# Output projection one token tile at a time in both column halves, all weight units resident, normalisation on VectorE, late modulation moved into the feed-forward

## The chip, the core and the metric

The kernel runs on one core of a Trainium2 chip. The metric is the device time of one execution in microseconds. The engines are named as the profile names them: PE (TensorE's matmuls) and PEld (its weight loads), DVE (VectorE), ACT (ScalarE), POOL (GpSimd) and SP (SyncE, whose queue issues nearly all of the kernel's DMAs).

## What is computed

Two post-norm layers of a trunk over 640 tokens: 512 latent tokens and 128 context tokens. `D_MODEL` is 1024 and the feed-forward width `D_FF` is 2816. Cut to what matters here:

```python
def trunk_layer(x, mod, w_in, w_out, ..., ln_g, ln_b, w_ffn_in, w_ffn_out, ctx):
    shift_m, scale_m, gate_m, shift_f, scale_f, gate_f = jnp.split(mod.astype(x.dtype), 6, axis=-1)
    z = (x * (1 + scale_m) + shift_m) @ w_in
    o, k_c, v_c, s_d, s_h = token_mixers(z, ...)
    x = layer_norm(ALPHA * x + gate_m * (o @ w_out), ln_g[0], ln_b[0])
    gt, up = jnp.split((x * (1 + scale_f) + shift_f) @ w_ffn_in, 2, axis=-1)
    x = layer_norm(ALPHA * x + gate_f * ((jax.nn.silu(gt) * up) @ w_ffn_out), ln_g[1], ln_b[1])
    return x, k_c, v_c, s_d, s_h
```

`mod` is SiLU(cond) times `w_mod[l]` plus a bias: six vectors of 1024 numbers for a layer, one set for the latent and one for the context tokens. The change touches the stretch from `o @ w_out` to the start of the feed-forward, once in each layer.

## The kernel before

The 640 tokens are five tiles of 128 (`tau` 0 to 4). Every product is float32-like: a weight unit is loaded as `raw` (512 KB, a ring of three buffers in the pool `praw`), ACT casts its high part into `hl`, DVE forms the low part (`hl<-raw,hl`), and PE makes three passes (high x high, high x low, low x high). The ring of `hl` units has four buffers. A matmul, a cast or a DMA is put on its engine's queue by a scheduler, which reorders the program as written; each engine then runs its queue strictly in order. Which order came out can be listed, and is shown below.

**Output projection** (`pop`). A result tile is 128 tokens by 512 columns, so there are two column halves (`nh` 0 and 1) of five tiles. A half needs four weight units `us0` or `us1` (each two of the eight 128-row slabs `k`), and a tile is 24 matmuls. Before, half 0 runs first for all five tiles, in two goes of two units each; then half 1 runs tile by tile, with one step of `mods_late` ahead of each product.

**Residual and normalisation.** After each half of a tile, `residual` runs on DVE: `rt` = psum x gate, `r` = ALPHA x + `rt`, and the statistics `st`. After half 1 `ln_next` makes the modulated normalised rows `xma`. For tiles 0 to 2 (`SHARED[0][CUR[0]]` is 3 in both layers) ACT applies the statistics, DVE multiplies by the row vector `sc` and POOL adds the row vector `sh` in two halves; for tiles 3 and 4 DVE does all of it in two passes (lines 542 and 543). `ffn_T` then transposes `xma` on PE (`pta`), ACT and DVE write its high and low part to `xT`.

**Sums for the feed-forward.** The input product of the feed-forward is done by seven block products instead of eight on halves of the tokens (`HT` = 320) and of `D_MODEL`. It needs three sums of `xT` blocks, which `ffn_sums` makes in `fA` and `fS` (ACT, DVE and POOL) and stores in `SX`.

**Feed-forward.** For each of the 22 blocks `f`, `pair_a(f)` makes the gate products `pfa` from one weight unit (`gate_unit`), and `pair_b(f)` the others (`pfc`, `pfb`, `pfd`) from two loads, `g_` and `u_`, out of which POOL and DVE make the differences `t`. `AHEAD` = 4 gate blocks go ahead. The blocks come in parts (0-4, 4-8, ...), and after each part its output product `pfo` is added to `r`.

**Late modulation** (`mods_late`, line 1395). Vector 5 (`gate_f`) of this layer and, in layer 0, vector 0 of the next one are worked out here: eight `raw` loads of `w_mod` for a vector, and eight matmuls (`psm`, as the profile counts them) for a load. A step takes two loads.

## Time and profile before

| what | value |
|---|---|
| time, median of 3 runs | 2103.04 us (2100.37 to 2107.04) |
| profiled execution: its own time | 2098.58 us |
| span of its core | 2096.8 us |
| PE busy | 1915.2 us, 91% |
| PEld busy | 1681.5 us, 80% |
| DVE busy | 1440.6 us, 69% |
| POOL busy | 891.6 us, 43% |
| ACT busy | 791.2 us, 38% |
| granted TensorE clock, mean | 0.956 |

The profile is of one execution, whose time is 1.8 us above its span. Times in rows count from the start of the span. Layer 0's output projection begins at 531 us and its feed-forward's first output product at 682 us; layer 1's projection begins at 1558 us.

### The profile page before, as it was taken

What the parts mean: (1) busy time and instruction counts of PE and PEld (TensorE: products, weight loads), DVE (VectorE), ACT (ScalarE), POOL (GpSimd) and SP (SyncE); (2) the same over time, 40 slices, a digit from 0 to 9 for tenths busy, and PEclk for the clock granted to TensorE, in tenths of its full rate; (3) what the DMA queues carried; (4) which work ended last, traced back from release to release, by engine and by line L of the source; (5) the groups of instructions that cost most, each with busy time, mean ns of one, the idle gap of its engine ahead of it and who ended that gap; (6) DMA issues with size and microseconds to landing.
All of it is one profiled execution on the core that took longest, in us unless ns stands there. A gap on an engine that the chain in (4) does not pass through costs nothing. (4 is left out here: it accounts for less than half of the span.)

```text
span 2096.8 us, 37785 instructions
## 1 busy us (share of the span) xinstructions
PE 1915.2 (91%) x14914; PEld 1681.5 (80%) x14914; DVE 1440.6 (69%) x2516; ACT 791.2 (38%) x1564; POOL 891.6 (43%) x988
## 2 busy tenths in 40 slices
PE   7999997778988999999989999977799799999996
PEld 5988986657768899989989979755687779989895
DVE  5458534778588866667666784368857897667676
ACT  3542322647143334333336323135742434334331
POOL 0375234766142132435156924357642411432445
PEclk7999998899999999999999999989889999999998
DMA  9423215872653322222434342377235232223221
GB/s 303 112 74 123 90 64 149 225 221 74 211 181 89 114 81 91 71 81 81 133 94 131 108 135 67 102 186 231 87 130 159 84 111 91 71 81 97 76 76 76
DMA packets 243399, 249.36 MB, mean 119 GB/s; under 512 B 19370, under 2 KB 190358, under 8 KB 243222
## 3 DMA queue, kind: packets, MB, share of 16 engines
q1 hardware_dynamic: 221046, 227.27, 35.0%
q10 hardware_dynamic: 22176, 19.67, 3.6%
q8 instruction: 118, 1.93, 0.4%
q14 instruction: 59, 0.48, 0.1%
HBM read 218.72 MB, written 28.18 MB: 118 GB/s over the span
## 5 line engine op out<-in xcount | busy, mean ns | idle before, releaser
L176 DVE TENSOR_TENSOR hl<-raw,hl 128x1024 fp32r<-128x1024 f32 (+1 forms) x210 | 280.1, 1337 | 88.7 <-ACT hl L273 70.9
L173 PE MATMUL pfo<-hl,ha 128*128 128x512 f32 x1320 | 312.9, 395 | 1.5 <-ACT hl L273 0.8
L173 PEld LDWEIGHTS pfo<-hl,ha 128*128 128x128 f32 x1320 | 246.1, 187 | 60.7 <-DVE ft L176 1.2
L176 POOL TENSOR_TENSOR r<-r,ft 128x512 f32<-128x512 f32 x96 | 143.0, 1510 | 248.4 <-DVE ft L176 247.7
L176 POOL TENSOR_TENSOR t<-raw 128x512 f32<-128x512 f32 x44 | 67.9, 1543 | 338.7 <-DMA raw<-in_w_ffn_in_dram 145.4
L173 PE MATMUL pfa<-xT,hl 128*128 128x320 f32 x1056 | 175.3, 316 | 8.7 <-DVE ms L176 3.5
L273 ACT CAST hl<-raw 128x1024 fp32r<-128x1024 f32 (+2 forms) x122 | 125.5, 1036 | 147.8 <-DMA raw<-in_w_ffn_out_dram 45.9
L173 PE MATMUL pfc<-sx,hl 128*128 128x320 f32 x1056 | 172.2, 311 | 9.4 <-ACT hl L1550 8.2
L173 PEld LDWEIGHTS pfa<-xT,hl 128*128 128x128 f32 x1056 | 162.7, 193 | 12.4 <-ACT sx L1513 3.9
L173 PEld LDWEIGHTS pfc<-sx,hl 128*128 128x128 f32 x1056 | 160.4, 189 | 13.0 <-ACT hl L1550 9.0
L1550 ACT CAST hl<-raw 128x1024 fp32r<-128x1024 f32 x88 | 92.1, 1051 | 207.7 <-PE pfo L173 104.4
L173 PE MATMUL paq<-xT,hl 128*128 128x320 f32 x768 | 123.1, 317 | 0.6 <-ACT az L1238 0.6
L173 PE MATMUL pop<-hl,xT 128*128 128x512 f32 x480 | 118.0, 402 | 0.7 <-ACT ae_p L1131 0.7
L173 PEld LDWEIGHTS paq<-xT,hl 128*128 128x128 f32 x768 | 115.7, 190 | 3.4 <-issue 1.2
L173 PEld LDWEIGHTS pop<-hl,xT 128*128 128x128 f32 x480 | 89.6, 191 | 24.9 <-issue 4.7
L176 POOL TENSOR_TENSOR hK<-hK,hT 64x256 f32<-64x256 f32 x120 | 90.6, 755 | 33.4 <-PE ph L173 27.7
L176 DVE TENSOR_TENSOR ft<-pfo,lg 128x512 f32<-128x512 f32 x96 | 63.8, 683 | 55.5 <-PE pfo L173 44.1
L173 PE MATMUL pfd<-xT,h 128*128 128x320 f32 x528 | 87.7, 316 | 9.9 <-DVE u L176 9.9
L176 DVE TENSOR_TENSOR t<-raw,t 128x512 f32<-128x512 f32 x88 | 73.9, 840 | 33.1 <-POOL t L176 33.0
L173 PE MATMUL pbq<-xT,hl 128*128 128x320 f32 x576 | 89.9, 313 | 1.0 <-DVE hl L176 0.4
L173 PEld LDWEIGHTS pfd<-xT,h 128*128 128x128 f32 x528 | 81.4, 193 | 11.4 <-issue 8.7
L173 PE MATMUL pfb<-sx,hl 128*128 128x320 f32 x528 | 88.6, 310 | 0.6 <-DVE hl L176 0.6
(409 smaller groups left out, 4213.0 us busy)
## 6 DMA issues: line engine op xcount, KB each, us to landing
raw<-in_w_ffn_in_dram SPq DMA_DIRECT2D x96, 512.0 KB
raw<-in_w_mod_dram SPq DMA_DIRECT2D x80, 512.0 KB
raw<-in_w_in_dram SPq DMA_DIRECT2D x56, 512.0 KB
raw<-in_w_ffn_out_dram SPq DMA_DIRECT2D x44, 512.0 KB
pc<-in_w_mod_dram SPq DMA_DIRECT2D x8, 1024.0 KB
raw<-in_w_out_dram SPq DMA_DIRECT2D x16, 512.0 KB
qksc<-az SPq DMA_DIRECT2D x16, 320.0 KB
qkhi<-azs SPq DMA_DIRECT2D x16, 256.0 KB
```

The costliest lines, as they stand in the source:

```text
L173: nc.tensor.matmul(out, lhsT, rhs, start=start, stop=stop, **kw)
L176: return eng.tensor_tensor(out, a, b, op)
L273: A.copy(hl[:, 0, :kt * n], raw[:, :kt * n])
L1550: A.copy(tile_[:, 0, :n], raw)
```

## The change

- Half 0 takes one unit (`u0[:1]`) for all five tiles first. Then the loop goes tile by tile: the other three units of half 0 for tile `i`, and half 1 for tile `i - 1`.
- The four units of half 1 no longer wait for the four of half 0 to leave the `hl` ring: three of them are put in buffers `w0` to `w2`, whose memory the three sums `SX` take over afterwards. `SX` becomes three tiles, and `ffn_sums` runs for both pieces behind the last tile.
- The half-1 products have one more psum bank (`n=QQ + RR + PP1`); `mods_late` no longer has one of its own there.
- `mods_late` moves into the feed-forward: one step after each `pair_a` of the first four, then one after each `pair_b` (layer 0 has eight steps, layer 1 four).
- Two gate units instead of one are loaded ahead, behind tile 4's half 0.
- `SHARED[0]` becomes (0, 0): DVE alone does the normalisation of all five tiles, in two passes each.
- The feed-forward's `s` and `g` buffers and `xtra` are allocated ahead of `ha`.

```diff
--- before.py
+++ after.py
@@ -245,7 +245,7 @@
     AFFINE = ((V, V), (G, G))
-    SHARED = [(3, 3), 3]
+    SHARED = [(0, 0), 3]
@@ -267,7 +267,8 @@
         raw, _ = raw_unit(src, kt, n)
         seq = [x_ for x_ in HL["seq"] for _ in range(x_[2])]
         hp_, tag, n_ = seq[HL["i"] % len(seq)]
-        hl = hp_.tile([P, 2, 1024], F32R, tag=tag, bufs=n_, name="hl")
+        w_ = 4 * HT if tag[0] == "w" else 1024
+        hl = hp_.tile([P, 2, w_], F32R, tag=tag, bufs=n_, name="hl")
         HL["i"] += 1
         with behind():
             A.copy(hl[:, 0, :kt * n], raw[:, :kt * n])
@@ -1455,7 +1456,7 @@
         psum_banks(True)
-        psum_phase(n=QQ + RR + PP1[:1], m=PP1[1:], t=PP2)
+        psum_phase(n=QQ + RR + PP1, t=PP2)
         rc, rp = pool(f"R{l}", "right")
         r = [rp.tile([P, D], F32, name=f"r{l}_{tau}") for tau in range(NT)]
         st = [rp.tile([P, 2, 6], F32, name=f"st{l}_{tau}") for tau in range(NT)]
@@ -1464,15 +1465,16 @@
         lg = rp.tile([P, D], F32, name=f"lg{l}")
         lb_ = rp.tile([P, D], F32, name=f"lb{l}")
         hx, hxp = pool(f"hx{l}", "left")
-        SX = hxp.tile([P, 3, 2, 4, HT], F32R, name=f"sx{l}")
         sc_, sp = pool(f"S{l}", "left")
         fA = sp.tile([P, 4, HT], F32, name=f"fa{l}")
         fS = sp.tile([P, 4, HT], F32, name=f"fs{l}")
         HL["seq"], HL["i"] = [(phl, "hl", 4)], 0
         lc, lp = pool(f"L{l}", "left")
         WB[0] = 3
-        pre = [lp.tile([P, D], F32, tag=t_, name=f"{t_}{l}") for t_ in ("sc0", "sh0", "sc1", "sh1")]
-        gm = [lp.tile([P, D], F32, name=f"gm{l}_{j}") for j in range(2)]
+        pre, gm = [], []
+        for j in range(2):
+            pre += [lp.tile([P, D], F32, tag=f"{t_}{j}", name=f"{t_}{j}{l}") for t_ in ("sc", "sh")]
+            gm.append(lp.tile([P, D], F32, name=f"gm{l}_{j}"))
         def residual(ps, gate, x, rt, nh, stt):
             cs = slice(nh * 512, (nh + 1) * 512)
...
@@ -1533,15 +1535,6 @@
         rowload(None, ln_b[l, 0], None, lb_)
         rows = affine_rows(lp, l, 4, 3, pre)
         Wi, Wo = w_ffn_in[l], w_ffn_out[l]
-        pss = [psS("n", f"pop{l}_0_{tau}") for tau in range(NT)]
-        us0 = [(rowunit(w_out[l], 2 * i, 2, 0, 512), [2 * i, 2 * i + 1]) for i in (2, 3, 0, 1)]
-        for tau in range(NT):
-            gemm_N(pss[tau], 512, xT, tau, us0[:2], last=False)
-        for tau in range(NT):
-            gemm_N(pss[tau], 512, xT, tau, us0[2:], first=False)
-            residual(pss[tau], gm[tau >= LT][:, :512], r[tau], r[tau], 0, st[tau])
-        us1 = [(rowunit(w_out[l], 2 * i, 2, 512, 512), [2 * i, 2 * i + 1]) for i in (2, 3, 0, 1)]
-
         def load_col(c0, f):
             return raw_unit(Wi[:, c0 + f * P:c0 + f * P + P].rearrange("(k p) n -> p k n", p=P), KT, P)[0]
@@ -1563,24 +1556,45 @@
                 raws[f] = (g_, load_col(DFF, f))
             gts[f] = in_two(g_, 1024, hl_tile())
-        gate_unit(0)
-        late_m = mods_late()
+
+
+        def out_unit(i, nh):
+            return rowunit(w_out[l], 2 * i, 2, nh * 512, 512), [2 * i, 2 * i + 1]
+
+        pss = [psS("n", f"pop{l}_0_{tau}") for tau in range(NT)]
+        u0 = [out_unit(i, 0) for i in (2, 3, 0, 1)]
         for tau in range(NT):
-            for _ in range(2):
-                next(late_m, 0)
-            ps = psS("n", f"pop{l}_1_{tau}")
-            gemm_N(ps, 512, xT, tau, us1)
-            j = 0 if tau < LT else 1
-            residual(ps, gm[j][:, 512:], r[tau], r[tau], 1, st[tau])
-            AFTER[:] = ln_next(lp, r[tau], st[tau], mv, rs, rows[j], xT, tau, f"a{l}_{tau}", ffn_T)
-            if tau >= 3:
-                ffn_sums(*((0, 4 * P - HT) if tau == 3 else (4 * P - HT, HT)))
+            gemm_N(pss[tau], 512, xT, tau, u0[:1], last=False)
+        u1 = [out_unit(2, 1)]
+        HL["seq"], HL["i"] = [(hxp, f"w{x}", 1) for x in range(3)], 0
+        u1 += [out_unit(i, 1) for i in (3, 0, 1)]
+        HL["seq"], HL["i"] = [(phl, "hl", 4)], 0
+        for i in range(NT + 1):
+            if i < NT:
+                gemm_N(pss[i], 512, xT, i, u0[1:], first=False)
+                residual(pss[i], gm[i >= LT][:, :512], r[i], r[i], 0, st[i])
+            if i == NT - 1:
+                gate_unit(0)
+                gate_unit(1)
+            if i:
+                tau, j = i - 1, int(i > LT)
+                ps = psS("n", f"pop{l}_1_{tau}")
+                gemm_N(ps, 512, xT, tau, u1[1:] + u1[:1])
+                residual(ps, gm[j][:, 512:], r[tau], r[tau], 1, st[tau])
+                AFTER[:] = ln_next(lp, r[tau], st[tau], mv, rs, rows[j], xT, tau, f"a{l}_{tau}", ffn_T)
+        SX = [hxp.tile([P, 2, 4, HT], F32R, tag=f"w{x}", bufs=1, name=f"sx{l}_{x}") for x in range(3)]
+        ffn_sums(0, 4 * P - HT)
+        ffn_sums(4 * P - HT, HT)
         close(lc)
         close(sc_)
         psum_phase(g_n=PP1 + QQ + RR, t_m=PP2)
         fc, fp = pool(f"F{l}", "right")
+        ring = [[fp.tile([P, w_], F32, tag=f"{t_}{x}", bufs=1, name=f"{t_}{x}_{l}") for t_, w_ in (("s", HT), ("g", NTOK))]
+                for x in range(2)]
+        xtra = fp.tile([P, 2048], F32, tag="hb", bufs=1, name=f"xtra{l}")
+        ring += [[xtra[:, x * 960:x * 960 + HT], xtra[:, x * 960 + HT:x * 960 + 960]] for x in range(AHEAD - 2)]
         ha = fp.tile([P, 2, 4, NTOK], F32R, name=f"ha{l}")
         h_ = lambda xi, k: ha[:, xi, k]
         sc_, sp = pool(f"V{l}", "left")
...
@@ -1607,11 +1621,11 @@
             gt_ = gts.pop(f)
             a_ = psS("g", f"pfa{l}_{f}")
             prod(a_, gt_, 0, "11")
-            if 2 <= f < AHEAD:
-                s1, sg = xtra[:, (f - 2) * 960:(f - 2) * 960 + HT], xtra[:, (f - 2) * 960 + HT:(f - 1) * 960]
+            if f < AHEAD:
+                s1, sg = ring[f]
             else:
-                s1 = fp.tile([P, HT], F32, tag="s1", bufs=2, name=f"s1_{l}_{f}")
-                sg = fp.tile([P, NTOK], F32, tag="sg", bufs=2, name=f"sg{l}_{f}")
+                s1, sg = (fp.tile([P, w_], F32, tag=f"{t_}{f % 2}", bufs=1, name=f"{t_}{l}_{f}")
+                          for t_, w_ in (("s", HT), ("g", NTOK)))
             A.copy(s1, a_[:, :HT])
             prod(a_, gt_, 4, "12", start=False)
             A.activation(sg[:, :HT], a_[:, :HT], AF.Silu)
@@ -1659,14 +1673,16 @@
             A.activation(sg[:, HT:], u2, AF.Silu)
             return out(1, u4)
-        xtra = fp.tile([P, 2048], F32, tag="hb", bufs=1, name=f"xtra{l}")
+        late_m = mods_late()
         for f in range(AHEAD):
             pair_a(f)
+            next(late_m, 0)
         for part, (f0, f1) in enumerate(FF_PARTS):
             nk = f1 - f0
             last = part == len(FF_PARTS) - 1
             for f in range(f0, f1):
                 end = pair_b(f, f - f0)
+                next(late_m, 0)
                 if AHEAD - 1 <= f < NFF - 1:
                     pair_a(f + 1)
                 if part == 0:
```

Where instructions now stand is seen on three queues. On DVE in layer 0, these are the rows around the first use of a half-1 product (`rt<-pop_1_0`); the first number after `pop` is the half, the second the tile. Before:

```order
L176 TENSOR_TENSOR rt<-pop_0_3_6113,gm_0_6095 128x512
L1481 SCALAR_TENSOR_TENSOR r_3_6068<-r_3_6068,rt 128x512
L1482 BN_STATS st_3_6073<-r_3_6068 128x6
L176 TENSOR_TENSOR hl<-raw,hl 128x1024
L176 TENSOR_TENSOR rt<-pop_0_4_6114,gm_1_6096 128x512
L1481 SCALAR_TENSOR_TENSOR r_4_6069<-r_4_6069,rt 128x512
L1482 BN_STATS st_4_6074<-r_4_6069 128x6
L176 TENSOR_TENSOR hl<-raw,hl 128x1024
L176 TENSOR_TENSOR rt<-pop_1_0_6327,gm_0_6095 128x512
L1481 SCALAR_TENSOR_TENSOR r_0_6065<-r_0_6065,rt 128x512
L176 TENSOR_TENSOR rt<-pop_1_1_6407,gm_0_6095 128x512
L1482 BN_STATS st_0_6070<-r_0_6065 128x6
```

and now:

```order
L176 TENSOR_TENSOR rt<-pop_1_0_6228,gm_0_6092 128x512
L176 TENSOR_TENSOR rt<-pop_0_2_6111,gm_0_6092 128x512
L1483 SCALAR_TENSOR_TENSOR r_0_6065<-r_0_6065,rt 128x512
L1483 SCALAR_TENSOR_TENSOR r_2_6067<-r_2_6067,rt 128x512
L1484 BN_STATS st_0_6070<-r_0_6065 128x6
L176 TENSOR_TENSOR rt<-pop_1_1_6299,gm_0_6092 128x512
L1484 BN_STATS st_2_6072<-r_2_6067 128x6
L176 TENSOR_TENSOR rt<-pop_0_3_6112,gm_0_6092 128x512
L531 BN_AGGR mv_6075<-st_0_6070 128x2
L1483 SCALAR_TENSOR_TENSOR r_1_6066<-r_1_6066,rt 128x512
L1483 SCALAR_TENSOR_TENSOR r_3_6068<-r_3_6068,rt 128x512
L532 TENSOR_SCALAR rs_6076<-mv_6075 128x1
```

The residuals of half 0 for tiles 2, 3 and 4 stood ahead of the first half-1 residual; now they stand behind it, between the residuals of half 1 (tile 4's follows behind these rows), and `xma` is written by lines 543 and 544, which are lines 542 and 543 of before.

On PE in layer 1, these are the rows from the last of half 0's first tiles to the end of `pop_1_0`. Before:

```order
L173 MATMUL pop_0_3_16347<-hl,xT_14419 128x512 x12
L173 MATMUL pop_1_0_16561<-hl,xT_14419 128x512 x12
L173 MATMUL pop_1_1_16641<-hl,xT_14419 128x512 x6
L173 MATMUL pop_1_0_16561<-hl,xT_14419 128x512 x2
L173 MATMUL pop_1_1_16641<-hl,xT_14419 128x512 x4
L173 MATMUL pop_1_0_16561<-hl,xT_14419 128x512 x6
L173 MATMUL pop_1_1_16641<-hl,xT_14419 128x512 x5
L173 MATMUL pop_1_0_16561<-hl,xT_14419 128x512
L173 MATMUL psm_5_16536<-raw,cm 32x256 x4
L173 MATMUL pop_1_0_16561<-hl,xT_14419 128x512 x3
```

and now:

```order
L173 MATMUL pop_0_1_16337<-hl,xT_14412 128x512 x18
L173 MATMUL pop_1_0_16455<-hl,xT_14412 128x512 x12
L173 MATMUL pop_0_2_16338<-hl,xT_14412 128x512 x18
L173 MATMUL pop_1_1_16526<-hl,xT_14412 128x512 x12
L173 MATMUL pop_1_0_16455<-hl,xT_14412 128x512 x2
L173 MATMUL pop_1_1_16526<-hl,xT_14412 128x512 x2
L173 MATMUL pop_0_3_16339<-hl,xT_14412 128x512 x2
L173 MATMUL pop_1_0_16455<-hl,xT_14412 128x512 x10
L173 MATMUL pop_1_1_16526<-hl,xT_14412 128x512 x10
L173 MATMUL pop_0_3_16339<-hl,xT_14412 128x512 x16
L173 MATMUL pop_1_2_16597<-hl,xT_14412 128x512 x24
L173 MATMUL pop_0_4_16340<-hl,xT_14412 128x512 x4
```

All 120 matmuls of half 0 stood ahead of `pop_1_0`; now 16 of tile 3's and 4 of tile 4's stand behind it, and the modulation's `psm` is gone from there.

On SP in layer 0, these are the loads from the last unit of `w_out` to the first loads of `w_ffn_out`. Before:

```order
L254 DMA raw<-in_w_out_dram 128x2x512
L254 DMA raw<-in_w_ffn_in_dram 128x8x128
L254 DMA raw<-in_w_mod_dram 128x1024 x11
L482 DMA modrow_426<-ms_5_6403 4x256 x2
L470 DMA mbias<-in_b_mod_dram 4x256 x2
L254 DMA raw<-in_w_mod_dram 128x1024 x5
L254 DMA raw<-in_w_ffn_in_dram 128x8x128 x3
L482 DMA modrow_427<-ms_0_6564 4x256 x2
L470 DMA mbias<-in_b_mod_dram 4x256 x2
L254 DMA raw<-in_w_ffn_in_dram 128x8x128 x10
```

and now (10 of the rows that follow the same load):

```order
L254 DMA raw<-in_w_out_dram 128x2x512
L254 DMA raw<-in_w_ffn_in_dram 128x8x128 x2
L254 DMA raw<-in_w_mod_dram 128x1024 x4
L254 DMA raw<-in_w_ffn_in_dram 128x8x128
L254 DMA raw<-in_w_mod_dram 128x1024 x2
L254 DMA raw<-in_w_ffn_in_dram 128x8x128
L254 DMA raw<-in_w_mod_dram 128x1024 x2
L254 DMA raw<-in_w_ffn_in_dram 128x8x128 x2
L254 DMA raw<-in_w_mod_dram 128x1024
L483 DMA modrow_426<-ms_5_6765 4x256 x2
L471 DMA mbias<-in_b_mod_dram 4x256 x2
L254 DMA raw<-in_w_mod_dram 128x1024
```

The 16 loads of `w_mod` stood between the first gate unit's load and the other three; now they are spread between the gate units' loads and, after these rows, go on as two loads of `w_mod` to each two of `w_ffn_in`.

## Rows read from the trace of the kernel before

**Rows 1.** Busy time by stretch: us, PE, PEld, DVE, ACT, POOL, clock, DMA share, GB/s

```profile
531.00:571.20 40.20, 40.20 (x181) 31.86 (x182) 18.00 (x30) 6.34 (x14) 3.36 (x6) 1.00 0.65 223
571.20:629.20 58.00, 49.82 (x326) 36.02 (x326) 50.68 (x69) 22.92 (x34) 25.75 (x17) 0.94 0.58 182
594.30:629.20 34.90, 26.72 (x199) 20.11 (x199) 31.38 (x39) 16.70 (x27) 12.85 (x8) 0.90 0.69 212
1597.00:1654.70 57.70, 46.22 (x273) 35.75 (x271) 50.86 (x68) 22.91 (x35) 29.02 (x17) 0.96 0.37 110
1622.80:1654.70 31.90, 20.42 (x122) 18.15 (x120) 29.48 (x35) 15.99 (x27) 16.94 (x7) 0.93 0.27 76
```

**Rows 2.** PE's timeline: start, us, line, operation, result<-inputs, count, idle before it

```profile
548.23 21.94 PE L173 MATMUL pop<-hl,xT 128*128 128x512 f32 x93
570.10 0.64 PE L173 MATMUL psm<-raw,cm 128*32 128x256 f32 x8
...
631.82 0.56 PE L173 MATMUL pfc<-sx,hl 128*128 128x320 f32 x2 [1.46 <-ACT hl L1550]
...
681.99 22.67 PE L173 MATMUL pfo<-hl,ha 128*128 128x512 f32 x96 [0.79 <-ACT hl L273]
...
1656.48 0.90 PE L173 MATMUL pfc<-sx,hl 128*128 128x320 f32 x2 [6.76 <-ACT hl L1550]
```

**Rows 3.** DVE's timeline, in the same columns

```profile
550.46 0.69 DVE L1482 BATCH_NORM_STATS2 st<-r 128x6 f32<-128x512 f32 x1
...
571.21 0.69 DVE L176 TENSOR_TENSOR rt<-pop,gm 128x512 f32<-128x512 f32 x1 [6.95 <-PE pop L173]
571.94 0.69 DVE L1481 SCALAR_TENSOR_TENSOR r<-r,rt 128x512 f32<-128x512 f32 x1
...
588.17 1.21 DVE L176 TENSOR_TENSOR xma<-xma,sc 128x1024 f32<-128x1024 f32 x1
...
629.19 1.40 DVE L176 TENSOR_TENSOR t<-raw,t 128x512 f32<-128x512 f32 x2
...
1597.00 0.69 DVE L176 TENSOR_TENSOR rt<-pop,gm 128x512 f32<-128x512 f32 x1 [3.93 <-PE pop L173]
...
1654.66 1.41 DVE L176 TENSOR_TENSOR t<-raw,t 128x512 f32<-128x512 f32 x2
```

**Rows 4.** DVE's groups, 571.2 to 629.2: shapes, count | busy, mean ns | idle before

```profile
L176 DVE TENSOR_TENSOR hl<-raw,hl 128x1024 fp32r<-128x1024 f32 x4 | 6.0, 1489 | 0.0
L1481 DVE SCALAR_TENSOR_TENSOR r<-r,rt 128x512 f32<-128x512 f32 x5 | 4.5, 903 | 0.0
L176 DVE TENSOR_TENSOR xma<-xma,sc 128x1024 f32<-128x1024 f32 x3 | 4.0, 1330 | 0.8 <-ACT xma L536 0.8
L543 DVE SCALAR_TENSOR_TENSOR xma<-xma,rs,sh 128x1024 f32<-128x1024 f32 x2 | 2.6, 1282 | 0.4 <-POOL rs L176 0.4
```

**Rows 5.** The same view of DVE, 1597 to 1654.7

```profile
L176 DVE TENSOR_TENSOR xma<-xma,sc 128x1024 f32<-128x1024 f32 x3 | 4.8, 1603 | 2.3 <-ACT xma L536 2.3
```

**Rows 6.** The matmuls `psm` alone, up to the end of the last `pop`

```profile
570.00:594.30 24.30, 4.24 (x48) 1.17 (x48) 0.00 (x0) 1.00 0.40 130
1590.00:1622.80 32.80, 5.52 (x64) 1.49 (x64) 0.42 (x1) 1.00 0.48 149
```

**Rows 7.** SP's timeline: load issues

```profile
608.06 0.38 SPq L254 DMA_DIRECT2D raw<-in_w_ffn_in_dram  x1
...
630.66 0.37 SPq L254 DMA_DIRECT2D raw<-in_w_ffn_in_dram  x1
...
676.76 0.39 SPq L254 DMA_DIRECT2D raw<-in_w_ffn_out_dram  x1
```

**Rows 8.** ACT's timeline: the cast behind the first of these loads

```profile
613.48 1.05 ACT L1550 CAST hl<-raw 128x1024 fp32r<-128x1024 f32 x1 [0.61 <-DMA raw<-in_w_ffn_in_dram]
```

**Rows 9.** POOL's timeline

```profile
579.06 6.48 POOL L176 TENSOR_TENSOR xma<-xma,sh 128x512 f32<-128x512 f32 x4 [2.35 <-PE psm L173]
...
634.50 1.43 POOL L176 TENSOR_TENSOR t<-raw 128x512 f32<-128x512 f32 x1 [5.78 <-DMA raw<-in_w_ffn_in_dram]
```

More of the change, by code (lines that the diff above doesn't have):

```diff
@@ L1514, in two @@
                 tt(V, lo, src, hi.bitcast(F32), ALU.subtract)
-            two(s_, SX[:, 0, 0, :, a:b], SX[:, 0, 1, :, a:b])
+            two(s_, SX[0][:, 0, :, a:b], SX[0][:, 1, :, a:b])
             tt(G, f_, x(0, 0), f_, ALU.subtract)
@@ L1520, in ffn_sums @@
                 tt(V, s_, s_, x(xi, 0), ALU.subtract)
-            two(s_, SX[:, 1, 0, :, a:b], SX[:, 1, 1, :, a:b])
+            two(s_, SX[1][:, 0, :, a:b], SX[1][:, 1, :, a:b])
             two(f_, xT[:, 0, 0:4, HT + a:HT + b], xT[:, 1, 0:4, HT + a:HT + b])
@@ L1524, in ffn_sums @@
             tt(V, s_, s_, x(1, 4), ALU.add)
-            two(s_, SX[:, 2, 0, :, a:b], SX[:, 2, 1, :, a:b])
+            two(s_, SX[2][:, 0, :, a:b], SX[2][:, 1, :, a:b])
         S.dma_start(r[0], xin(l, 0))
@@ L1591, in tile_trunk @@
               "22": lambda xi, k: xT[:, xi, 4 + k, HT:], "s3": lambda xi, k: xT[:, xi, k, HT:],
-              "s1": lambda xi, k: SX[:, 0, xi, k], "s2": lambda xi, k: SX[:, 1, xi, k],
-              "s4": lambda xi, k: SX[:, 2, xi, k]}
+              "s1": lambda xi, k: SX[0][:, xi, k], "s2": lambda xi, k: SX[1][:, xi, k],
+              "s4": lambda xi, k: SX[2][:, xi, k]}
         def prod(ps, w, k0, x, start=True):
```

## The prediction, as written before the changed kernel had run

> **What bounds the kernel now.** The page says PE: 91% busy. That is an average, so the first view I read is the busy time of each engine over the stretches that the change touches [rows 1]. In the first of them (531 to 571 us) PE is busy all 40.2 us and DVE only 18.0. From 571.2 to 629.2 it is the other way: DVE works 50.7 of 58.0 us, and after the last `pop` product (594.3) 31.4 of 34.9, while PE has 26.7 and a granted clock of 0.90. Layer 1 shows the same: DVE 50.9 of 57.7, and at the end 29.5 of 31.9 against PE's 20.4 at 0.93.
>
> The timelines say where DVE's run begins and ends. It begins when `pop_1_0` ends: `rt` starts at 571.21 after 6.95 us idle (1597.00 after 3.93 in layer 1), and it ends with `t` at 629.19 (1654.66) [rows 3]. PE's `pfc`, the first product that needs the sums and the second weight units, follows at 631.82 and 1656.48, 2.6 and 1.8 us behind the start of that `t` [rows 2]. From the output product at 682 on PE runs on without a gap (96 matmuls in 22.67), so what is won or lost up to there stays in the end time. The stretch to look at is therefore the one from `pop_1_0` to `pfc`, DVE ends it, and before it DVE has some 22 us to spare.
>
> The profiled execution's own time is 2098.58 us, 4.5 below the median of the runs, inside what they spread over. I make the sum against the profile and carry the difference over to the median.
>
> **Resident units.** PE has no gap in the stretch where half 1 had to wait for half 0's units (40.2 of 40.2) [rows 1]: 93 matmuls take 21.94 us, 0.236 each, back to back [rows 2]. So the third bank and the resident units bring PE nothing there. Their effect is the order of the products.
>
> **Start of DVE's run.** In layer 0 six more `pop` matmuls stand ahead of the end of `pop_1_0` (1.4 us) and one load's `psm` less (0.64 [rows 2]): 572.1 instead of 571.2, +0.9 with rounding. In layer 1, 20 matmuls of half 0 and one of another product now stand behind it (21 x 0.236 = 5.0) and one load's `psm` (0.6): 1591.4 instead of 1597.0, −5.6.
>
> **DVE's work in the run.** *Residuals.* Those of half 0 for tiles 2, 3 and 4 lay in DVE's idle time before 571. DVE takes its queue in order, and now they stand behind `rt<-pop_1_0`, so that cover is gone: three times `rt`, `r` and `st` at 0.69 each [rows 3], +6.2 per layer. What is late next is the normalised rows, hence the transposes and the sums. *Normalisation.* For three tiles two passes at 1.28 [rows 4] take the place of one at 1.21 when alone [rows 3]: 3 x (2.56 − 1.21) = +4.0. In return ACT's pass and POOL's six half adds (four took 6.48 [rows 9]) go, and with them what DVE pays for running beside POOL. In layer 0 the `xma` pass takes 1.33 instead of 1.21 (x3: 0.33), `r` 0.90 instead of 0.69 (x5: 1.07), and the low part `hl` 1.49 where it is about 1.22 alone (x4: 1.08, an estimate from the `xma` pass of the same size) [rows 3, 4]: −2.5. In layer 1 the `xma` pass alone gives 3 x (1.60 − 1.21) = 1.2 [rows 5], and with a share for `r` I take −1.8. Sum: +7.7 in layer 0, +8.4 in layer 1.
>
> The Trainium skill, page "SBUF — State Buffer", section "Who interferes with whom", says that DVE and GpSimd share one pair of SBUF ports under an exclusive lock. By that rule each of the six POOL adds could hold a two-input DVE instruction for its whole length, which is the last rival below; the lengthening in the rows is far smaller than the adds are long.
>
> Put together for layer 0: 572.1 + 50.7 + 7.7 = 630.5 if no wait is left, +2.6 gives `pfc` at 633.1. Of the 7.3 us that DVE now idles in the run, 0.8 is for ACT's `xma`, which goes [rows 4], and about 2 are waits for `pop`, which the moved residuals fill; with the other 4.5 it is 637.6. For layer 1: 1591.4 + 50.9 + 8.4 = 1650.7, +1.8 gives 1652.5; its idle 6.8 loses the 2.3 of `xma` [rows 5] and 0.7, and with the remaining 3.8 it is 1656.3. I choose near the lower ends, since other ready work now stands beside those waits: 634 (+2) and 1653.5 (−3).
>
> **The loads.** `raw` has three buffers. A load lands 3.8 us after its issue when little else runs (630.66 [rows 7] to POOL's start at 634.50 [rows 9]) and 5.4 when much does (608.06 to 613.48 [rows 7, 8]). Behind the last transposes nine loads now have to pass (five of `w_mod`, two gate units, `g_` and `u_`): three turns of the ring. With 1 us of queueing and the cast or `psm` a turn is 5.5 to 7, and the last adds POOL's `t` (1.43), DVE's (0.7) and ACT's cast (1.05): about 631 in layer 0 counted from 608, 634 to 636 with slow landings. So loads and DVE nearly tie there; layer 1 is alike, at 1651 to 1656.
>
> In layer 0 vector 0's eight loads then stand in the turns of `pair_b`, two to each `f`. A load of `w_ffn_in` holds its buffer for 3.84 and the chain POOL, DVE, ACT (1.43 + 1.40 + 1.05) and 1 of queueing, about 9; one of `w_mod` for 5.5. Four of them through three buffers are (18 + 11) / 3 = 9.7 us, 38.7 for four blocks. Now `pfc` to the first `w_ffn_out` load is 45 us (631.8 to 676.76) [rows 2, 7]. That load now stands behind vector 0's sum and stores, some 3 to 6 us more: 42 to 45, no loss. With landings of 5.4 a block is 11.8 and it comes to 50 to 53: +5 to +8, with the gate loads +9. I take +3, nearer to the unloaded row, since that one is from this very place. PE's own cost of these `psm` (8 x 0.64 = 5.1) goes beside those turns.
>
> **Clock.** The clock is 0.90 to 0.93 where PE waits between the products [rows 1]. Without `psm` to fill these waits PE is idle longer there and I price +0.5.
>
> **Nothing.** The second gate unit ahead, the banks and the order of the pools cost no instruction; the gate unit's cast goes beside the products of `pop`. The scheduler also shifts a few instructions of layer 1's mixers, at PE's pace in both; unknown, ±3 for the range.
>
> **Sum.** +2 − 3 + 3 + 0.5 = +2.5: 2101.1 for the profiled execution, 2105.5 at the median; I round to 2105. With both lower ends and no loss in the turns it is 2101, with both upper ends 2116.
>
> **The rivals.** *Faster: PE leads.* If the tail behind the last `pop` depends on that product and not on DVE's sum of work, `pfc` follows it. Up to that point six loads' `psm` leave PE in layer 0 (48 matmuls, 3.8 us) and eight in layer 1 (64, 5.1) [rows 2, 6], and the tail stays as long as now: −8.9, and if the ring of loads hides vector 0's turns, 2103 − 8.9 = 2094. For it: PE is busy without a gap up to `pop_1_0`, and the third bank and resident units take every wait from the products. Against it: DVE's 31.4 of 34.9 behind the last product. It decides if DVE finds the three residuals' 6.2 us in waits, which now total 7.3 and 6.8.
>
> *Slower: the loads pace.* If landings are 5.4 us in both chains, `pfc` comes at about 635 (+3) and in layer 1 no earlier than now (0 instead of −3), and the turns cost 9, with the clock: about +13, 2117. For it: vector 0's loads stood where the ring had time, now each `pair_b` needs twice the loads through the same three buffers. Against it: DMA share is 0.6 to 0.7 before `pfc` but loads after it landed in 3.84. It decides if a block's turn goes over 11.5 us.
>
> *It does not bring anything.* Layer 0's later start and layer 1's earlier one cancel; that is my forecast.
>
> *Faster: the shared port.* If POOL's adds held DVE for their whole length, six of 1.6 us would be 9.7 per layer, against 2.5 and 1.8 counted above: another −15, about 2090. Against it are the same rows: `xma` lengthened by 0.1 to 0.4 only. The rule on the lock is the page "SBUF — State Buffer" as above.
>
> **How the numbers follow.** A measurement can tell about 0.3% (6.3 us) from no change. Forecast 0.45, all within it; loads pace 0.28, slower; PE leads 0.20 and the port 0.07, faster. The range runs from 2092 (a little under PE leads) to 2117 (loads pace) and takes in the mixers' ±3; outside lie most of the port's case and the half of the loads' case that is dearer, together about 0.2. The forecast's own range is 2099 to 2110.
>
> **What the profile after would show.** Right: DVE idle until about 572 and 1591 before `rt<-pop_1_0`, then residuals of both halves mixed; `pfc` some 103 us after layer 0's `pop` begins at 531 (101 now) and 3 earlier than now in layer 1; blocks of `pair_b` in layer 0 at about 11 us each with PE waiting for loads, and the first `pfo` some 5 us later than now. Wrong: DVE with clear waits between the last `pop` and `pfc` would speak for PE or loads instead of its sum of work; `pfc` before 628 for PE leads; `raw` named as the releaser on ACT and POOL ahead of every `pfc` for the loads. What would upset it all is a wait that I put at nothing, most likely of `hl` units for their ring at the start of the projection.

## The result, and the profile after

The changed kernel is slower: 2122.59 us (median of 6 runs, 2119.78 to 2129.89) against 2107.37 for the kernel before (6 runs, 2100.37 to 2112.76) on the same chips. The ratio is 1.0086, 95% interval [1.0063, 1.011], so some 18 us (the two medians differ by 15.2). That is above the range of the prediction (2092 to 2117), and above its slower rival, the loads' pace, at 2117.

The profiled execution took 2123.51 us. These rows of its trace are the matmuls of three products in each layer (count, ns at least/median/most, first and last start); the window was cut at 1100 us, so the first, third and fifth are layer 0's.

```profile
L173 PE MATMUL pop<-hl,xT x240: 388/394/796, 536.9 to 595.5; 128*128 128x512 f32 x120
L173 PE MATMUL pop<-hl,xT x240: 387/389/499, 1579.6 to 1636.0; 128*128 128x512 f32 x120
L173 PE MATMUL pfc<-sx,hl x528: 302/309/634, 643.8 to 1055.1; 128*128 128x320 f32 x176
L173 PE MATMUL pfc<-sx,hl x528: 302/309/637, 1679.9 to 2077.8; 128*128 128x320 f32 x176
L173 PE MATMUL pfo<-hl,ha x660: 387/394/793, 702.2 to 1078.2; 128*128 128x512 f32 x165
L173 PE MATMUL pfo<-hl,ha x660: 388/394/506, 1721.5 to 2102.3; 128*128 128x512 f32 x165
```

From them I take two lengths for each layer, which all experiments below are read by: from the first `pop` to the first `pfc` (layer 0: 643.8 − 536.9 = 106.9; before 100.8), and from there to the last `pfo` (layer 0: 434.4; before 424.5). Layer 1 went from 98.9 to 100.3 and from 420.9 to 422.4. Together these are +18.9 us, about the 18 of the ratio. Ahead of layer 0's first `pop` both kernels run the same instructions in the same order, and the 5.9 us between 531.0 and 536.9 are of these two executions (last section). Between layer 0's last `pfo` and layer 1's first `pop` stand layer 1's token mixers, 501.3 us before and 501.4 now. Their instructions are the same, but the scheduler put about a quarter of DVE's 685 there at another place in the queue, and the 18 kernels of the table below have 14 different orders there. One sign of it: the five `hK` of one pass ran in one go on DVE before (first row) and now have another instruction among them (the next three):

```profile
1390.21 3.44 DVE L607 TENSOR_SCALAR hK<-hf 128x512 f32<-128x512 f32 x5 [0.78 <-DMA aks<-qksc]
```

```profile
1416.61 2.05 DVE L608 TENSOR_SCALAR hK<-hf 128x512 f32<-128x512 f32 x3
1418.59 0.14 DVE L1135 RECIPROCAL ari<-ar 128x1 f32<-128x1 f32 x1
1418.65 1.50 DVE L608 TENSOR_SCALAR hK<-hf 128x512 f32<-128x512 f32 x2
```

That stretch has a column of its own in the table below.

Where layer 0's 6 us ahead of `pfc` are is seen in DVE's timeline, around the start and the end of its run:

```profile
579.57 1.29 DVE L176 TENSOR_TENSOR rt<-pop,gm 128x512 f32<-128x512 f32 x2 [14.52 <-PE pop L173]
580.77 1.28 DVE L1483 SCALAR_TENSOR_TENSOR r<-r,rt 128x512 f32<-128x512 f32 x2
...
585.70 1.28 DVE L543 SCALAR_TENSOR_TENSOR xma<-r,mv,sc 128x1024 f32<-128x1024 f32 x1
...
636.60 0.69 DVE L176 TENSOR_TENSOR sx<-fs,sx 128x512 fp32r<-128x512 f32 x1 [2.12 <-ACT sx L1515]
638.45 0.42 DVE L176 TENSOR_TENSOR ms<-psm,mbias 128x256 f32<-128x256 f32 x1 [1.17 <-PE psm L173]
642.02 2.37 DVE L176 TENSOR_TENSOR t<-raw,t 128x512 f32<-128x512 f32 x2 [3.14 <-POOL t L176]
```

The run starts 42.7 us after the first `pop` (before 40.2) and has its last sum done at 637.3, 100.4 after it. Until there DVE waits 3.2 us in all. Then it waits 3.14 us for POOL, and POOL's own row says for what: a load.

```profile
640.73 1.26 POOL L176 TENSOR_TENSOR t<-raw 128x512 f32<-128x512 f32 x1 [15.42 <-DMA raw<-in_w_ffn_in_dram]
```

Layer 1 has the same wait, longer. DVE's last sum and its `t`:

```profile
1669.54 0.69 DVE L176 TENSOR_TENSOR sx<-fs,sx 128x512 fp32r<-128x512 f32 x1
...
1678.10 2.36 DVE L176 TENSOR_TENSOR t<-raw,t 128x512 f32<-128x512 f32 x2 [5.53 <-POOL t L176]
```

In the kernel before, `t` at 629.19 followed DVE's sums without a wait [rows 3]. Why the load comes late, SP's queue tells, its issues and then what it waited for from 560 to 643 us (total, times, longest):

```profile
559.87 4.44 SPq L254 DMA_DIRECT2D raw<-in_w_ffn_in_dram  x2
565.07 53.19 SPq L254 DMA_DIRECT2D raw<-in_w_mod_dram  x4
618.37 1.64 SPq L254 DMA_DIRECT2D raw<-in_w_ffn_in_dram  x1
...
633.90 2.69 SPq L254 DMA_DIRECT2D raw<-in_w_ffn_in_dram  x2
```

```profile
SPq L254 <- DVE hl L176: 51.9, 6, 44.9
SPq L254 <- PE psm L173: 16.0, 7, 6.0
```

Both gate units sit in `raw` and wait for their low parts on DVE. So SP stands still for 44.9 us behind the first load of `w_mod`, and the second and third go out 15 us after the last `pop`:

```profile
610.37 1.46 SPq L254 DMA_DIRECT2D raw<-in_w_mod_dram  x2
```

The windows show it as a DMA share of 0.00 (the columns are those of [rows 1]):

```profile
578.00:595.70 17.70, 17.70 (x77) 14.19 (x76) 16.13 (x27) 0.00 (x0) 3.04 (x2) 1.00 0.00 1
595.70:643.80 48.10, 33.00 (x209) 25.59 (x207) 40.55 (x52) 20.79 (x33) 15.52 (x9) 0.78 0.43 132
```

Behind `pfc` the blocks of layer 0 go to 702.18 instead of 681.99 [rows 2]. PE's last row there and SP's queue ahead of it:

```profile
702.18 1.22 PE L173 MATMUL pfo<-hl,ha 128*128 128x512 f32 x2 [5.14 <-ACT hl L274]
```

```profile
682.46 2.58 SPq L254 DMA_DIRECT2D raw<-in_w_ffn_in_dram  x2
689.48 0.34 SPq L515 DMA_DIRECT2D aff<-modrow  x1
...
694.59 1.07 SPq L483 DMA_DIRECT2D modrow<-ms  x2
695.70 0.53 SPq L471 DMA_DIRECT2D mbias<-in_b_mod_dram  x1
696.33 0.84 SPq L515 DMA_DIRECT2D aff<-modrow  x2
697.34 0.39 SPq L254 DMA_DIRECT2D raw<-in_w_ffn_out_dram  x1
```

The rows for layer 1 (`aff`, made in buffers of the same `raw` ring) need vector 0. Its store `modrow<-ms` is issued at 694.59, they wait for it, and the first load of `w_ffn_out` goes out behind them, 53.5 us after `pfc` (before 45 [rows 2, 7]). These small transfers, from the first `aff` at 689.48 to that load at 697.34, are called the chain below; they take SP 7.9 us. In the kernel before the chain stood there too, from 665.33 to 676.76, but vector 0 was long done.

### The profile page after: what moved, and what is told of

Same layout as the page of the kernel before. It is cut to its first block, busy times and chain, and to the rows that moved or that the text cites. A ratio compares the mean times of both kernels' runs of the same rounds, so it can differ in the third digit from the quotient of the medians.

```text
span 2121.7 us, 37750 instructions
## 1 busy us (share of the span) xinstructions
PE 1935.8 (91%) x14914; PEld 1698.8 (80%) x14914; DVE 1439.0 (68%) x2516; ACT 783.9 (37%) x1558; POOL 871.4 (41%) x976
## 5 line engine op out<-in xcount | busy, mean ns | idle before, releaser
L176 DVE TENSOR_TENSOR hl<-raw,hl 128x1024 fp32r<-128x1024 f32 (+1 forms) x210 | 274.2, 1311 | 92.1 <-ACT hl L274 71.2
L173 PEld LDWEIGHTS pfc<-sx,hl 128*128 128x128 f32 x1056 | 161.8, 191 | 15.2 <-ACT hl L1543 10.5
L1543 ACT CAST hl<-raw 128x1024 fp32r<-128x1024 f32 x88 | 92.2, 1051 | 209.2 <-PE pfo L173 102.2
L176 POOL TENSOR_TENSOR hK<-hK,hT 64x256 f32<-64x256 f32 x120 | 90.8, 757 | 40.1 <-PE ph L173 34.4
L173 PEld LDWEIGHTS pbq<-xT,hl 128*128 128x128 f32 x576 | 87.5, 194 | 2.6 <-issue 0.8
## 6 DMA issues: line engine op xcount, KB each, us to landing
raw<-in_w_ffn_in_dram SPq DMA_DIRECT2D x96, 512.0 KB
raw<-in_w_mod_dram SPq DMA_DIRECT2D x80, 512.0 KB
raw<-in_w_in_dram SPq DMA_DIRECT2D x56, 512.0 KB
raw<-in_w_ffn_out_dram SPq DMA_DIRECT2D x44, 512.0 KB
raw<-in_w_out_dram SPq DMA_DIRECT2D x16, 512.0 KB
```

Source lines behind the costliest of these rows:

```text
L173: nc.tensor.matmul(out, lhsT, rhs, start=start, stop=stop, **kw)
L176: return eng.tensor_tensor(out, a, b, op)
L1543: A.copy(tile_[:, 0, :n], raw)
```

## The experiments

Each kernel ran with the kernel before on the same chip, five rounds. The table stands first, since the texts point to it; times are us from the profiles as above, the ratio is to the kernel before with its 95% interval.

| kernel | L0 pop to pfc | L0 pfc to last pfo | L0 last pfo to L1 pop | L1 pop to pfc | L1 pfc to last pfo | ratio |
|---|---|---|---|---|---|---|
| before | 100.8 | 424.5 | 501.3 | 98.9 | 420.9 | 1 |
| changed | 106.9 | 434.4 | 501.4 | 100.3 | 422.4 | 1.0086 [1.0063, 1.011] |
| e1, modulation back | 106.3 | 423.2 | 497.5 | 102.2 | 421.8 | 0.9999 [0.9985, 1.0013] |
| e2, shared normalisation back | 107.0 | 433.6 | 498.8 | 104.0 | 423.4 | 1.0075 [1.0047, 1.0102] |
| e3, before + modulation moved | 99.0 | 433.8 | 510.3 | 101.9 | 422.6 | 1.0053 [1.0035, 1.007] |
| e4, before + DVE normalisation | 102.1 | 423.6 | 501.9 | 99.0 | 421.2 | 0.9992 [0.9976, 1.0008] |
| e6, no loads of w_mod | 103.7 | 422.5 | 504.4 | 95.7 | 421.6 | 0.9987 [0.9972, 1.0001] |
| e7, a quarter of psm | 104.6 | 429.8 | 491.9 | 100.2 | 423.7 | 1.0011 [0.9996, 1.0025] |
| e8, vector 0 in blocks 4 to 7 | 106.7 | 439.8 | 501.5 | 101.5 | 422.5 | 1.0113 [1.0099, 1.0127] |
| e10, and vector 5 back | 101.5 | 439.3 | 506.0 | 100.0 | 422.5 | 1.0109 [1.0094, 1.0123] |
| e11, rows a part later | 105.2 | 425.7 | 507.8 | 100.8 | 421.2 | 1.0043 [1.003, 1.0056] |
| f1, e3 + rows later | 100.8 | 426.2 | 497.0 | 100.0 | 421.9 | 1.0016 [1.0001, 1.003] |
| f2, before + rows later | 104.4 | 421.9 | 502.1 | 99.9 | 422.7 | 0.9986 [0.9975, 0.9997] |
| e12, modulation in the mixers | 97.5 | 423.9 | 505.0 | 96.3 | 421.2 | 0.9981 [0.9967, 0.9996] |
| e13, before + vector 0 in the mixers | 99.3 | 424.3 | 500.2 | 99.4 | 422.2 | 0.9981 [0.9968, 0.9995] |
| e14, before + modulation in the mixers | 98.5 | 422.9 | 512.0 | 96.7 | 422.6 | 1.004 [1.0026, 1.0054] |
| e15, vector 5 in pop, 0 in the mixers | 102.7 | 423.6 | 507.9 | 96.4 | 422.2 | 1.004 [1.0023, 1.0057] |
| f3, e12 + rows later | 97.7 | 422.9 | 499.0 | 92.8 | 420.9 | 0.997 [0.9954, 0.9987] |

How far to trust one profile: the kernel before and f2 run the same instructions in the same order up to the first `pfc` and show 100.8 and 104.4 in the first column. A difference under 4 us in the columns up to `pfc` says little. In the third column, layer 1's mixers, four pairs of kernels have the same order, but for two or three instructions at most: before and e4, e1 and e13, e2 and f1, e6 and e8. Within a pair the column differs by 0.6 to 2.9 us, over all kernels by 20 (491.9 to 512.0). Part of that is the execution, since layer 0's mixers differ by up to 10 us with one order (last section). So the order in layer 1's mixers may change the time by some us, which no run tests by itself, and a ratio can hold that without the change itself being its cause. The second column lies within 421.9 to 426.2 for every kernel but those that load vector 0 right ahead of the rows made of it, which are at 429.8 to 439.8.

**Which part of the change costs.** Theory L: the loads of the moved modulation. Theory D: the order of the residuals and the normalisation on DVE. Four kernels undo or do one part.

e1, the modulation put back:

```diff
-        psum_phase(n=QQ + RR + PP1, t=PP2)
+        psum_phase(n=QQ + RR + PP1[:1], m=PP1[1:], t=PP2)
...
             if i:
                 tau, j = i - 1, int(i > LT)
+                for _ in range(2):
+                    next(late_m, 0)
                 ps = psS("n", f"pop{l}_1_{tau}")
...
             pair_a(f)
-            next(late_m, 0)
```

> The changed kernel with the late modulation put back into the projection (two steps ahead of each half-1 product, its own psum bank). Theory L (the loads of w_mod now pass the ring of three behind the gate units and pace pfc and the first blocks): 2107 us, at the kernel before, and from the first pfc to the first pfo of layer 0 about 50 us again. Theory D (the order of residuals and the normalisation on DVE cost the time): stays above 2117.

e2, `SHARED = [(3, 3), 3]` in the changed kernel:

> The changed kernel with ACT, DVE and POOL sharing the normalisation of tiles 0 to 2 again. Theory L: no change against the changed kernel, 2120 to 2124. Theory D: 4 us back in each layer, 2114. If the shared port is what matters the time goes up by some 5 us, to 2127.

e3, the kernel before with the lines of `mods_late` as in the change and nothing else of it:

> The kernel before with the late modulation alone moved into the feed-forward (and its psum bank given to the half-1 products). Theory L: 2120, the whole loss, and layer 0's pfc to pfo about 58 us. Theory D: 2107, no loss.

e4, `SHARED = [(0, 0), 3]` in the kernel before:

> The kernel before with the normalisation by DVE alone. Theory L: 2107, no change. Theory D: 2113 to 2116, slower by half of the loss. Shared port: faster, 2098 to 2102.

e1 is back at the kernel before (0.9999), e2 stays with the changed one, e4 is no different from the kernel before. By the times theory D falls and theory L stands: the move of the modulation costs 11 us alone (e3) and 18 in the new order (changed against e1). The stretches say it less plainly. Between the profiles of the changed kernel and e1, 11.2 us come back behind `pfc` in layer 0 (434.4 to 423.2) and 3.9 in layer 1's mixers, but ahead of `pfc` in layer 0 nothing does (106.3). There DVE ends the stretch in e1: its `t` follows the last sum without a wait for a load.

```profile
637.28 1.41 DVE L176 TENSOR_TENSOR t<-raw,t 128x512 f32<-128x512 f32 x2
```

So the 6 us ahead of `pfc` are not the moved loads alone. With the old order the first column is 99.0 and 100.8 when the modulation is moved (e3, f1); with the new order it is 101.5 to 107.0 wherever loads of `w_mod` stand near it, 97.5 and 97.7 when all stand in the mixers (e12, f3), and 103.7 in e6 below, without the loads. Why the new order takes these loads worse is not shown. SP's long wait for the gate units is not the reason by itself: e12 has one of 41.8 us in its 97.5 (the view from 545 to 640 us).

```profile
SPq L254 <- DVE hl L176: 67.2, 7, 41.8
```

**Loads or PE's time.** e6 keeps the matmuls and drops the loads, e7 keeps the loads and drops most matmuls.

```diff
-                raw, _ = raw_unit(w_mod[l][k * P:(k + 1) * P, i * D:(i + 1) * D].unsqueeze(1), 1, D)
+                raw = late if late is not None else raw_unit(w_mod[l][k * P:(k + 1) * P, i * D:(i + 1) * D].unsqueeze(1), 1, D)[0]
...
-            yield from modulation(l, (5,))
+            yield from modulation(l, (5,), lb_)
```

> The changed kernel, whose late modulation makes all its matmuls but loads nothing: each reads the resident row of ln_b in place of a load of w_mod, so gate_f of each layer and the first shift of layer 1 are other numbers. If the loads in the ring of three are the cost: 2103 to 2107, layer 0's pfc to pfo at 50 us. If PE's time for these matmuls is the cost: 2118 to 2122. If the order of the residuals costs the 6 us ahead of pfc in layer 0, that part stays (107 us from the first pop to the first pfc) whatever the loads do.

```diff
-                for g in range(4):
+                for g in range(4 if late is None or k == 0 else 1):
```

> The changed kernel with all loads of w_mod, but seven of eight loads of a late vector feed one matmul of four, so three quarters of the late modulation's result hold one load's part of the sum only. If the loads are the cost: 2120 to 2123, no change. If PE's time is: 24 loads at 0.64 us, of which 21 keep a quarter, give 10 us back: 2112.

Without the loads the kernel is at 0.9987, all of the loss gone, and layer 1 is 3 us better than before ahead of `pfc`. So PE's 15 us of `psm` cost nothing by themselves (24 loads at 0.64). But e7 is at 1.0011, where theory L said no change, and that expectation failed. Its stretches give back some 7 us in layer 0 and nothing in layer 1. The rest of its 16 us shows where the edit does not reach: layer 1's mixers, in another order, took 491.9 where the changed kernel has 501.4. So 9.5 us of it may be that order and not the matmuls. That the matmuls matter while the loads are there fits SP's rows: a load's buffer comes free only when its `psm` has run, in PE's strict order. For the second load of a step in a block this was 655.97 (issue) to 663.95 (end of `psm`), 8 us, where I had put 5.5.

```profile
655.97 0.34 SPq L254 DMA_DIRECT2D raw<-in_w_mod_dram  x1
```

```profile
661.10 0.63 PE L173 MATMUL psm<-raw,cm 128*32 128x256 f32 x4
661.65 1.74 PE L173 MATMUL pfd<-xT,hl 128*128 128x320 f32 x10
663.32 0.63 PE L173 MATMUL psm<-raw,cm 128*32 128x256 f32 x4
```

**Where vector 0 stands.** e8 moves its four steps from blocks 0 to 3 to blocks 4 to 7, and the rows made of it to the next part; e10 puts vector 5 back into the projection as well.

```diff
                 end = pair_b(f, f - f0)
-                next(late_m, 0)
+                if part:
+                    next(late_m, 0)
...
-            if part == 0 and l + 1 < DEPTH:
+            if part == 1 and l + 1 < DEPTH:
                 affine(l + 1, 1, 0, (l, 1), praw, "raw", 3)
```

> The changed kernel with the four steps of vector 0 moved from blocks 0 to 3 to blocks 4 to 7 of layer 0's feed-forward, and the rows made of it one part later. If they cost because block 0 to 3 had to pass four loads each with the next transfers waiting behind: pfc to pfo of layer 0 back at 50 us, 2114 in all. If the ring paces any block with four loads, the 8 us only move behind the first pfo: 2120 to 2123.

> The changed kernel with vector 5 back in the projection (one step ahead of each of the first four half-1 products) and vector 0 in blocks 4 to 7. If both places of the loads cost: 2105, as with the whole modulation back. If blocks 4 to 7 pay for vector 0: 2113. If the new order gains once the loads are out of its way: 2098 to 2102.

In neither did the time come back: 1.0113 and 1.0109, no better than the changed kernel. e8 came nearer to its second expectation, that the time only moves, though that said 2123 at most, and e10 missed all of its own. The first `pfo` comes 40.1 us after `pfc` in e8, but the time comes back behind it (439.8 in all). The trace shows a wait like the one in the changed kernel at the end of the next part:

```profile
779.22 21.16 PE L173 MATMUL pfo<-hl,ha 128*128 128x512 f32 x78 [3.78 <-ACT hl L274]
```

The wait had moved with the rows, which again stood right behind vector 0's last step. That gave a new theory: not the loads in the blocks, but the chain of small transfers behind vector 0 that holds SP's queue and the ring ahead of `w_ffn_out`. e11 moves the rows alone (the second half of e8's edit):

> The changed kernel with the rows made of vector 0 (the chain of small transfers through aff and modrow) one part later, the modulation's steps left where they are. If SP's queue holds the first w_ffn_out load back behind that chain and vector 0's stores: the 5.1 us wait ahead of the first pfo of layer 0 goes down to about 1, pfc to pfo 54 us, 2118. If the loads of the blocks alone set it, or the chain costs as much later: no change, 2120 to 2124.

1.0043, so 9 us of the 18 are back, and 434.4 is 425.7. The first `w_ffn_out` load no longer has the chain ahead of it, and `pfo` starts without a wait. SP and PE in e11:

```profile
685.67 0.37 SPq L254 DMA_DIRECT2D raw<-in_w_ffn_out_dram  x1
690.20 1.07 SPq L483 DMA_DIRECT2D modrow<-ms  x2
```

```profile
692.72 3.66 PE L173 MATMUL pfo<-hl,ha 128*128 128x512 f32 x15
```

It goes out 45.4 us after `pfc` (640.28), as in the kernel before. So the eight loads in the blocks, with the chain out of the way, cost about 1 us against the kernel before (425.7 and 424.5) and 4 against f2, where the chain is out of the way too (421.9). f1 is the same edit on e3, f2 on the kernel before:

> The kernel before with the late modulation moved, as in the run with that alone (1.0053), and the rows of vector 0 made one part later. If the chain right behind vector 0 is what cost there too: 8 us back, 1.001 of the kernel before, layer 0's pfc to the end of its feed-forward 425 us. If the loads in the blocks cost: 1.005 as in that run.

> The kernel before with only the rows of vector 0 made one part later. There vector 0 is long done when the chain is issued. If the chain costs only behind vector 0: no change, 2105, ratio 0.999 to 1.001. If it costs wherever it stands ahead of the first w_ffn_out load: 4 to 8 us faster, 0.997.

f1 goes from 1.0053 to 1.0016, as expected, and its second column from 433.8 to 426.2: the chain cost there too, some 8 us. f2 gains 0.14%, at the edge of what can be told, so where vector 0 was long done the chain costs little.

**What the rest is, and what the new order is worth.** e12 moves vectors 5 and 0 into the token mixers' modulation, so that projection and feed-forward load no `w_mod`; e14 does so in the kernel before, e13 there with vector 0 alone; e15 is the new order with vector 5 as in e10 and vector 0 in the mixers; f3 is e12 with the rows later.

```diff
         def mods():
...
+            yield from modulation(l, (5,))
             if l + 1 < DEPTH:
-                yield from modulation(l + 1, (1,))
+                yield from modulation(l + 1, (1, 0))
...
         def mods_late():
-            yield from modulation(l, (5,))
-            if l + 1 < DEPTH:
-                yield from modulation(l + 1, (0,))
+            yield from ()
```

> The changed kernel with all of the late modulation moved ahead into the token mixers, so that neither the projection nor the feed-forward has loads of w_mod. The order of the projection is then alone: from the run without loads 104 us at most from the first pop to pfc in layer 0 and 96 in layer 1, layer 0 behind pfc 49 to 50 us to pfo. In all 2098 to 2100 if PE's waits in the mixers (about 20% of their time) take the 24 loads and their matmuls (15 us); 2112 if the mixers pay for them.

> The kernel before with vector 0 alone moved ahead into the token mixers of layer 0. If its eight loads cost time in the projection: layer 0's first pop to pfc 97 instead of 101 and 2103 against 2105. If they stood in PE's waits there, as DVE sets the end: 101, 2107, or 2112 if the mixers pay.

> The kernel before with all of the late modulation moved ahead into the token mixers: beside the run of the changed kernel with the same move it tells what the order of the projection is worth by itself. By the sum of DVE's work the old order is 2 to 3 us better in layer 0 and 3 us worse in layer 1, so the two are equal within 2 us.

> The new order with vector 5 one step ahead of each of the first four half-1 products, and vector 0 in the token mixers of layer 0: no load of w_mod in the feed-forward. By the stretches of the run with vector 5 put back so, 101 us from pop to pfc in both layers, and 424 behind it in layer 0: 2104. If the place of vector 5 does not matter: as with all in the mixers, 2102 or less.

> The new order with all late modulation in the token mixers (0.9981 of the kernel before) and the rows of vector 0 one part later. If the chain costs only behind vector 0: 0.998 again. If it costs wherever it stands: 0.995, the fastest of all.

With no `w_mod` behind the mixers the new order is no slower than the kernel before: e12 is at 0.9981, between its two expectations, and f3 at 0.997 [0.9954, 0.9987], 2095.43 us (median of 9 runs) against 2103.03. f3 beats both kernels. In it DVE's `t` follows the last sum with no wait for a load:

```profile
635.25 0.69 DVE L176 TENSOR_TENSOR sx<-fs,sx 128x512 fp32r<-128x512 f32 x1 [0.68 <-ACT sx L1514]
635.86 1.41 DVE L176 TENSOR_TENSOR t<-raw,t 128x512 f32<-128x512 f32 x2
```

e13 gains 0.2% with vector 0 alone in the mixers. e14 and e15 missed: 1.004 where 1.000 or less was expected. The four stretches of e12 and e14 differ by 2 us in sum, their ratios by 0.6%, some 12 us. Of the other 10, 7 lie in layer 1's mixers, 512.0 in e14 and 505.0 in e12. e15 is alike: its four stretches are those of the kernel before in sum, its mixers take 507.9, and that is 6.6 of the 8 us that it lost. So what the new order is worth by itself stays open between the 2 us of the stretches and the 12 us of the medians, since no run has both orders with the same mixers.

## Why the prediction was wrong

- **Start of DVE's run.** Predicted 41.1 us after the first `pop` in layer 0 and 33.8 in layer 1; the trace has 42.7 and 31.8 (1611.44 − 1579.6). Right in both directions.
- **DVE's work in the run.** 50.7 + 7.7 = 58.4 busy was forecast for layer 0, 54.9 was measured up to `t` (579.57 to 642.02); in layer 1 59.3 and 56.2. Some 3 high in both. Two passes at 1.28 and `r` at 0.64 each show that there the lengthening beside POOL is gone.
- **Normalisation and the port.** I had +1.5 in layer 0, and the rival −15 in all. e4 shows 0.9992 [0.9976, 1.0008]: neither. The Trainium skill, page "SBUF — State Buffer", section "Who interferes with whom", calls the sharing of DVE's and GpSimd's ports an exclusive lock; the trace of the kernel before agrees more than I read from it: 1.33 and 1.60 are means of three passes [rows 4, 5], and "lengthened by 0.1 to 0.4 only" hides that a single pass can double. In layer 1 `xma` took 2.36 at 1605.82, beside two of POOL's adds (1604.57 to 1607.1), where the next took 1.23. Even so, taking these adds away was worth nothing in the time here.
- **Resident units and banks.** Nothing on PE, as said: 240 `pop` products took 58.6 us, and before 63.0 with 4.2 us of `psm` among them [rows 6].
- **Loads ahead of pfc.** This is the first of two steps that failed. "So loads and DVE nearly tie there" left no wait for a load, and the terms +2 and −3 went by DVE alone; measured were +6.1 and +1.4. DVE's sums ended 100.4 us after the first `pop` in layer 0 and 90.6 in layer 1 (1670.2 − 1579.6), and POOL's `t`, which waits for `g_` and `u_`, began at 103.8 and 97.2 (1676.81 − 1579.6). The loads end last, by 3.4 and 6.6. I had counted three turns from the last transposes, and had not seen that SP stands still until DVE has the low parts of the gate units, or that a buffer waits for PE to reach its `psm`. Without the loads (e6) the stretch is +2.9 and −3.2 against the kernel before, where the forecast was +2 and −3, as near as one profile can tell. So the two terms hold without the loads, and what ended last was the load. That the loads' new place alone did it is not shown, since e1 has 106.3 with the loads back in the projection.
- **Loads in the blocks.** This is the second. The prediction said that the `w_ffn_out` load "now stands behind vector 0's sum and stores, some 3 to 6 us more: 42 to 45, no loss", and took +3. It came 53.5 us after `pfc`, and the stretch is 9.9 us longer. I had the place right, and both parts too small. A block's turn is 12.7 us (issues at 644.45, 657.22, 669.81 and 682.46), where I chose 9.7 and had 11.8 as the loaded case; so the chain began 45.7 us after `pfc` and not 38.7. And the chain took 7.9, not 3 to 6: it is a wait on the last product of vector 0, in SP's order, with buffers of the ring taken meanwhile. The two make up the 53.5. What they cost is another matter: with the turns left at 12.4 and the chain moved, e11 gets 8.7 of the 9.9 back, so the chain right behind vector 0 was most of it.
- **Together.** The sum was +2.5, the stretches made +18.9. The loads ahead of `pfc` are 8.5 of what it missed, the loads in the blocks 6.9; the rest is layer 1 behind `pfc` (+1.5), less the 0.5 for the clock.
- **Clock.** +0.5 was priced. The granted clock from the last `pop` to `pfc` was 0.78 (before 0.90 [rows 1]). No run takes this apart from the waits.
- **The rivals.** "The loads pace" was given 0.28 and 2117. By its own test it was right, a turn over 11.5 us (12.7), and its price of 9 for the turns is near the 9.9; but that is in part luck, since e11 shows the chain and not the turns behind most of it. Ahead of `pfc` it had 0 for layer 1, near the +1.4, and +3 for layer 0, half of the 6.1. "PE leads" and the port stayed out: `pfc` came later, not earlier, and e4 gained nothing.

## What to carry to other kernels

Work that fills an engine's waits is not free to move, even off a stretch where that engine is not the bound: in this kernel what decided was where its loads stand in the ring, and what stands behind its result on the queue that issues the next weights. Before moving a step, follow its last store: where a queue issues in order, as SP's did here, whatever waits for that store holds every load behind it. About half of the loss here went with one line that issues the dependent rows later; with the loads made ahead in the mixers as well, the new order ended 0.3% faster than the kernel before. And where a scheduler orders the queues, an edit in one stretch can change another: compare the order and the length of the stretches that were not meant to change before a ratio is put down to the edit.

## What the runs showed of the hardware that was not expected

The instructions ahead of the projection in layer 0 are the same in the kernel before and the changed one, on all five engines. Yet the first `pop` comes at 531.0 and 536.9, and between 527.7 (e7) and 538.2 (e6) in the kernels whose PE and SP queues are the same up to there. The windows of the kernel before, the changed kernel and e7 from 318 to 425 us, in this order, show PE granted a different clock with about the same work, 0.87, 0.81 and 0.86:

```profile
318.00:425.00 107.00, 81.08 (x923) 64.92 (x923) 69.93 (x155) 45.50 (x128) 67.36 (x112) 0.87 0.67 190
```

```profile
318.00:425.00 107.00, 83.53 (x903) 67.74 (x906) 70.15 (x153) 44.69 (x125) 63.67 (x109) 0.81 0.66 183
```

```profile
318.00:425.00 107.00, 83.75 (x938) 67.12 (x934) 72.78 (x164) 46.04 (x130) 67.38 (x111) 0.86 0.67 192
```

So one profile's total is uncertain by up to 10 us from layer 0's mixers alone; the runs of the kernel before spread over 2097 to 2116. The level shows in the changed kernel's PE rows between the last `pop` and `pfc`: 20 `pfa` products took 5.70 us right behind waits of 3.68, 1.62 and 0.76 us, 0.285 each, and the next 24 took 3.79 us, 0.158 each. The granted clock is 0.51 in the first of these stretches and 1.00 in the second, the levels 1.2 and 2.4 GHz:

```profile
610.40:616.10 5.70, 5.70 (x22) 5.66 (x23) 4.75 (x5) 0.83 (x1) 1.98 (x2) 0.51 0.58 184
618.67:622.46 3.79, 3.79 (x32) 3.60 (x32) 3.76 (x6) 2.44 (x4) 0.94 (x1) 1.00 0.66 191
```

The products and the waits ahead of them:

```profile
602.92 1.94 PE L1494 MATMUL pta<-c_ident,xma 128*128 128x128 f32 x8 [3.68 <-DVE xma L544]
606.48 0.90 PE L173 MATMUL pfa<-xT,hl 128*128 128x320 f32 x2 [1.62 <-ACT hl L1543]
...
610.40 5.70 PE L173 MATMUL pfa<-xT,hl 128*128 128x320 f32 x20 [0.76 <-DVE hl L176]
...
618.67 3.79 PE L173 MATMUL pfa<-xT,hl 128*128 128x320 f32 x24
```
